# The order of the attention blocks in a two-layer decoder trunk: from 1, 2, 3 to 3, 2, 1

## The chip, the cores and the metric

One core of a Trainium2 chip runs the whole kernel in one launch. The metric is the device time of one execution in microseconds; the kernel before is given by the median of three runs. The engines are TensorE (PE in the profile, PEld for its weight loads), VectorE (DVE), ScalarE (ACT), GpSimd (POOL) and SyncE (SP, which issues the DMAs). Each engine works through its own instructions in a fixed order and waits at an instruction until what it needs is there.

## What is computed

The reference is a decoder trunk of two layers on 512 tokens of width 1024, in float32. Each layer normalises x, projects it once (W_in), gives the columns to three mixers, projects their joined outputs back (W_out), adds them to x, and then adds a squared-ReLU MLP. The mixers are a sparse attention of 8 heads of 64 with 2 key heads, an S5 recurrence and a Mamba-2 recurrence (SSD). The attention works by blocks of 128 queries; block b sees (b+1) x 128 keys:

```python
def attend(args):
    q_b, qi_b, wi_b, start = args
    idx_logits = jnp.einsum('bqhd,bsd->bqhs', qi_b, ki).astype(jnp.float32)
    score = jnp.einsum('bqh,bqhs->bqs', wi_b, jax.nn.relu(idx_logits))
    score = jnp.where(admissible[None], score, -jnp.inf)
    _, sel = lax.top_k(score, topk)      # topk = 128
...
    logits = jnp.where(valid[:, :, None, None, :], logits, -jnp.inf)
    p = jax.nn.softmax(logits, axis=-1).astype(v_sel.dtype)
    o = jnp.einsum('bqgrk,bqkgd->bqgrd', p, v_sel)
```

Blocks don't depend on each other. The 128 best of a block's keys are all of them in block 0, which needs no score.

## The kernel before, in words

Each layer has a stage of mixers and a stage of MLP. In layer 0 the mixers take about the first 330 us and the MLP the time to about 700; layer 1's mixers follow to about 955, then its MLP.

In the mixers' stage `mixers` starts nine or ten generators, each of which emits instructions and yields a cost: `trunk_in` (W_in, in parts kv, xa, qi, q, xb, u5, z; each weight slab is split into a high and a low half, L191 on ACT and L192 on DVE, and each product is three matmuls, L458 to L460), `keys`, `select`, `attention`, two of `recurrent` (S5 and SSD) and three of `out_proj`. `merge` (L1136) runs the generator whose virtual clock is least and adds the yielded cost, scaled by `PLAN`'s `pace`, with offsets from `start` and priorities from `prio`; a scheduler then orders each engine's instructions by priority. So the order in which generators emit blocks, and the places where they must wait for each other, set the order on every engine. PLAN has an entry for each layer.

`keys` (L1284) prepares the keys and then calls `index_scores` (L1058) for the blocks 1, 2, 3: ropes on the block's qi (L1002 to L1005, DVE), a split (L1042 ACT, L1043 DVE), transposes (L1046, PE), and for each of 8 heads two matmuls into `ix` (L1055), a ReLU `irl` (L1071, ACT) and a weighted sum into `isc` (L1073, L1074, L1076, DVE). `select` (L1296) takes the groups of blocks in PLAN's `top`; `topk_masks` (L1081) does 16 rounds for each group, in a round for each of its blocks one MAX8 (L1086) and one MATCH_REPLACE8 (L1087), and turns the scores into a mask (L1090). Layer 0 takes blocks 2 and 1 together and then 3; layer 1 takes 1, 2, 3 one by one.

`attention` (L1305) waits for q and the keys, takes the sums of squares of q (L983 ACT, L984 DVE) and their reciprocal roots, and then for each block ropes and transposes q, waits for the block's mask and calls `attend` (L1092): for each head two matmuls into `lg` (L1055), logits, mask and row maximum in one DVE instruction (L1107, into `pe` and `nmax`), exp (L1108, ACT), normalisation (L1111, L1115 on ACT, L1117 on DVE), then transposes `pTp` (L1123, PE), a copy `pT` (L1125, ACT), the product with v into `po` (L1128, PE), and its high and low half `mh` (L1132, ACT) and `ml` (L1133, DVE). The output projection of the attention part needs the `mh` and `ml` of all four blocks; its sums into x are L1373.

SSD's convolution (L844 to L858, DVE with ACT's tanh) makes `cv` and `CT` from the parts xa and xb; its transposes are L880 (`ssdT`), its scores L893 (`ssds`), both on PE. S5 ends in a gate: L762 and L777 on ACT, L763 and L779 on DVE.

Of the kernel before, what the change touches and what calls it, by code (L numbers as in the profile page):

```python
# [22 lines left out]
NB = S // P  # L23
# [35 lines left out]
PLAN = (  # L59
    {  # L60
        "w_order": ("kv", "xa", "qi", "q", "xb", "u5", "z"),
        "top": ((2, 1), (3,)),
        "out": (("s5",), ("att",), ("ssd",)),
        "serial": "no",
        "norm_act": (0,),
# [5 lines left out]
    },  # L71
    {
        "w_order": ("kv", "xa", "qi", "z", "u5", "q", "xb"),
        "top": ((1,), (2,), (3,)),
        "out": (("s5",), ("att",), ("ssd",)),
        "serial": "no",
        "norm_act": (0,),
# [143 lines left out]
class Net:  # L221
# [1064 lines left out]
    def keys(self, l, r):  # L1286
        while "ksb" not in r:
            yield None
        yield self.start["key"]
        r["K"] = yield from self.attn_keys(l, r["ksb"], self.rt)  # L1290
        for b in (1, 2, 3):
            while b not in r["qi"]:
                yield None
            yield from self.index_scores(b, r["qi"][b], r["K"], r["wi"][:, b], r["acc"])
# [10 lines left out]
    def attention(self, l, r):  # L1305
        nc = self.nc
        while len(r.get("q", ())) < NB or "K" not in r:
            yield None
        yield self.start["att"]
        q, rt = r["q"], self.rt  # L1310
        qms = self.s([P, NB, NH], tag="qms", bufs=1)
        qrs = self.s([P, NB, NH], tag="qrs", bufs=1)
        for b in range(NB):
            self.head_ms(qms[:, b], q[b], NH)
            yield self.pace["q"] * 0.7
        self.rsqrt(qrs.rearrange("p b h -> p (b h)"), qms.rearrange("p b h -> p (b h)"), NB * NH)
        nc.vector.tensor_scalar(qrs, qrs, -ATT_SCALE, None, ALU.mult)
        ah = [self.g(dt=F32R, name="mh") for _ in range(4)]
        al = [self.g(dt=F32R, name="ml") for _ in range(4)]
        for b in range(NB):  # L1320
            self.rope_q(q[b], *rt[2][b])
            qT = self.transpose_heads(q[b])
            yield self.pace["q"] * 2.5
            while b not in r["mask"]:
                yield None
            yield from self.attend(b, qT, r["K"], r["mask"][b], qrs[:, b], ah, al)
        for i in range(4):
            self.tap(f"at_{l}_{i}", ah[i].bitcast(F32)); self.tap(f"atl_{l}_{i}", al[i].bitcast(F32))
        r["mix"]["att"] = list(zip(ah, al))
# [252 lines left out]
```

## Time and profile before

| | us |
|---|---|
| median of 3 runs (lowest, highest) | 1332.07 (1332.04, 1332.51) |
| profiled execution | 1328.87 |
| its span | 1327.1 |
| PE busy in the span | 1218.0 (92%) |
| DVE busy | 885.2 (67%) |
| ACT busy | 549.2 (41%) |
| POOL busy | 169.7 (13%) |
| PE's share of the chain that ended last | 62% |
| DVE's share of it | 19% |

The busy shares are means over unlike stages: in the MLP stages PE has hardly a gap, and nothing else matters there. The chain of work that ended last is followed back from the last instruction, at each step to what released it. DVE's share of it lies in the mixers' stages. The profiled execution was 3.2 us shorter than the median of the runs; durations and places come from it.

### The profile page before, as it was taken

What the parts mean: (1) busy time and instruction counts of PE and PEld (TensorE: products, weight loads), DVE (VectorE), ACT (ScalarE), POOL (GpSimd) and SP (SyncE); (2) the same over time, 40 slices, a digit from 0 to 9 for tenths busy, and PEclk for the clock granted to TensorE, in tenths of its full rate; (3) what the DMA queues carried; (4) which work ended last, traced back from release to release, by engine and by line L of the source; (5) the groups of instructions that cost most, each with busy time, mean ns of one, the idle gap of its engine ahead of it and who ended that gap; (6) DMA issues with size and microseconds to landing.
All of it is one profiled execution on the core that took longest, in us unless ns stands there. A gap on an engine that the chain in (4) does not pass through costs nothing.

```text
span 1327.1 us, 17056 instructions
## 1 busy us (share of the span) xinstructions
PE 1218.0 (92%) x5708; PEld 977.1 (74%) x5708; DVE 885.2 (67%) x2024; ACT 549.2 (41%) x1128; POOL 169.7 (13%) x302
## 2 busy tenths in 40 slices
PE   5678957889999989999999989968999999999998
PEld 5566745458888868888888767754788888888887
DVE  5998999857886545665564699975475445444443
ACT  4245444664543533534443234455254233242331
POOL 2385100000796040000000000000000000000000
PEclk9889988899999999999999989978999999999999
DMA  5132220002567647677644634300323333333332
GB/s 189 40 88 70 74 74 24 9 1 72 148 213 257 214 146 252 224 262 230 227 149 137 219 120 124 120 17 1 111 88 97 101 97 96 96 96 99 100 110 81
DMA packets 139688, 161.64 MB, mean 122 GB/s; under 512 B 18768, under 2 KB 107600, under 8 KB 139600
## 3 DMA queue, kind: packets, MB, share of 16 engines
q1 hardware_dynamic: 139600, 160.55, 38.5%
q8 instruction: 45, 0.74, 0.2%
q14 instruction: 43, 0.35, 0.1%
HBM read 128.29 MB, written 31.03 MB: 120 GB/s over the span
## 4 chain that ended last, share of the span: by engine, by line
PE 62%; DVE 19%; issue 7%; POOL 6%; ACT 4%; DMA 1%; SPq 0%; ACTq 0%; DVEq 0%; POOLq 0%
PE pm L458 18%; PE pm L460 18%; PE pm L459 18%; PE po L1128 3%; DVE isc L1087 2%; DVE mx L1086 2%; DVE isc L1076 2%; PE pTp L1123 1%; DVE pe L1107 1%; DVE wlo L192 1%; DMA wraw<-in_w_in_dram 1%; POOL pt L660 1%; DVE cv L847 1%; ACT pe L1108 1%; POOL pt L661 1%
## 5 line engine op out<-in xcount | busy, mean ns | idle before, releaser
L192 DVE TENSOR_TENSOR wlo<-wraw,whi 128x512 fp32r<-128x512 f32 (+1 forms) x312 | 223.2, 718 | 243.0 <-ACT whi L191 241.4
L191 ACT ACTIVATE whi<-wraw 128x512 fp32r<-128x512 f32 (+1 forms) x312 | 194.1, 625 | 374.5 <-PE pm L459 236.9
L458 PE MATMUL pm<-xh,whi 128*128 128x512 f32 x640 | 252.4, 395 | 3.8 <-ACT q L1224 3.2
L460 PE MATMUL pm<-xh,wlo 128*128 128x512 f32 x640 | 250.1, 392 | 1.2 <-DVE wlo L192 1.2
L459 PE MATMUL pm<-xl,whi 128*128 128x512 f32 x640 | 250.9, 392 | 0.0
L460 PE MATMUL pm<-uh,wlo 128*128 128x512 f32 x512 | 199.7, 390 | 0.3 <-DVE wlo L192 0.3
L458 PE MATMUL pm<-uh,whi 128*128 128x512 f32 x512 | 199.6, 390 | 0.0
L459 PE MATMUL pm<-ul,whi 128*128 128x512 f32 x512 | 199.6, 390 | 0.0
L458 PEld LDWEIGHTS pm<-xh,whi 128*128 128x128 f32 x640 | 120.8, 189 | 30.8 <-ACT q L1224 3.9
L460 PEld LDWEIGHTS pm<-xh,wlo 128*128 128x128 f32 x640 | 120.6, 189 | 27.4 <-DVE wlo L192 2.0
L459 PEld LDWEIGHTS pm<-xl,whi 128*128 128x128 f32 x640 | 121.1, 189 | 24.2 <-issue 0.2
L460 PEld LDWEIGHTS pm<-uh,wlo 128*128 128x128 f32 x512 | 96.2, 188 | 20.8 <-DVE wlo L192 0.9
L459 PEld LDWEIGHTS pm<-ul,whi 128*128 128x128 f32 x512 | 96.3, 188 | 20.4 <-issue 0.4
L458 PEld LDWEIGHTS pm<-uh,whi 128*128 128x128 f32 x512 | 96.2, 188 | 20.3 <-issue 0.4
L458 PE MATMUL pm<-whi,xh 128*128 128x512 f32 (+1 forms) x176 | 67.4, 385 | 14.0 <-ACT xh L392 12.8
L460 PE MATMUL pm<-whi,xl 128*128 128x512 f32 (+1 forms) x176 | 66.6, 380 | 1.3 <-DVE xl L394 1.3
L459 PE MATMUL pm<-wlo,xh 128*128 128x512 f32 (+1 forms) x176 | 67.0, 381 | 0.5 <-DVE wlo L192 0.3
L1408 DVE TENSOR_TENSOR ul<-ur,uh 128x512 fp32r<-128x512 f32 x64 | 48.5, 758 | 21.0 <-ACT uh L1407 21.0
L1406 DVE SCALAR_TENSOR_TENSOR ur<-pm,ur 128x512 f32<-128x512 f32 x64 | 43.9, 686 | 23.0 <-ACT ur L1403 22.7
L1414 DVE TENSOR_TENSOR sq<-pm,r2b 128x512 f32<-128x512 f32 x64 | 44.1, 689 | 17.5 <-PE pm L460 17.5
L1407 ACT ACTIVATE uh<-ur 128x512 fp32r<-128x512 f32 x64 | 39.9, 624 | 30.7 <-DVE ur L1406 30.7
L1087 DVE MATCH_REPLACE8 isc<-mx,isc 128x256 f32<-128x256 f32 (+2 forms) x96 | 51.6, 541 | 0.0
(345 smaller groups left out, 1931.4 us busy)
## 6 DMA issues: line engine op xcount, KB each, us to landing
wraw<-in_w_up_dram SPq DMA_DIRECT2D x128, 256.0 KB, 2.8
wraw<-in_w_down_dram SPq DMA_DIRECT2D x128, 256.0 KB, 2.8
st<-shi SPq DMA_DIRECT2D x48, 256.0 KB, 2.9
st<-slo SPq DMA_DIRECT2D x48, 256.0 KB, 3.5
wlo<-st SPq DMA_DIRECT2D x48, 256.0 KB, 3.0
whi<-st SPq DMA_DIRECT2D x48, 256.0 KB, 2.8
wraw<-in_w_in_dram SPq DMA_DIRECT2D x32, 256.0 KB, 2.8
sraw<-in_w_in_dram SPq DMA_DIRECT2D x32, 256.0 KB, 3.9
```

The source lines that it names most:

```text
L191: nc.scalar.activation(hi, raw, AF.Copy)
L192: nc.vector.tensor_tensor(lo, raw, hi.bitcast(F32), ALU.subtract)
L458: nc.tensor.matmul(p, lh, rh, start=first, stop=False)
L459: nc.tensor.matmul(p, lh, rl, start=False, stop=False)
L460: nc.tensor.matmul(p, ll, rh, start=False, stop=last)
L1076: v.scalar_tensor_tensor(acc, r, wi[:, h:h + 1], acc, ALU.mult, ALU.add)
L1087: v.match_replace(acc, m8, acc, SENT)
L1128: nc.tensor.matmul(po[g_ * 64:g_ * 64 + 64], self.vt[:, kb, g_], pts[g_], start=kb == 0, stop=kb == b)
L1406: v.scalar_tensor_tensor(r, p, 0.0, r, ALU.max, ALU.mult)
L1407: nc.scalar.activation(h, r, AF.Copy)
L1408: v.tensor_tensor(lo, r, h.bitcast(F32), ALU.subtract)
L1414: v.tensor_tensor(t, d[1], rb, ALU.mult)
```

## The change

Three tables or loops get another order. Layer 0's `top` takes block 3 first and then 2 and 1 together; layer 1's takes 3, 2, 1; `keys` scores 3, 2, 1; `attention` takes 0, 3, 2, 1. Paces, starts, priorities and all shapes stay.

```diff
--- before.py
+++ after.py
@@ -59,7 +59,7 @@
 PLAN = (
     {
         "w_order": ("kv", "xa", "qi", "q", "xb", "u5", "z"),
-        "top": ((2, 1), (3,)),
+        "top": ((3,), (2, 1)),
         "out": (("s5",), ("att",), ("ssd",)),
         "serial": "no",
         "norm_act": (0,),
@@ -71,7 +71,7 @@
     },
     {
         "w_order": ("kv", "xa", "qi", "z", "u5", "q", "xb"),
-        "top": ((1,), (2,), (3,)),
+        "top": ((3,), (2,), (1,)),
         "out": (("s5",), ("att",), ("ssd",)),
         "serial": "no",
         "norm_act": (0,),
@@ -1288,7 +1288,7 @@
             yield None
         yield self.start["key"]
         r["K"] = yield from self.attn_keys(l, r["ksb"], self.rt)
-        for b in (1, 2, 3):
+        for b in (3, 2, 1):
             while b not in r["qi"]:
                 yield None
             yield from self.index_scores(b, r["qi"][b], r["K"], r["wi"][:, b], r["acc"])
@@ -1317,7 +1317,7 @@
         nc.vector.tensor_scalar(qrs, qrs, -ATT_SCALE, None, ALU.mult)
         ah = [self.g(dt=F32R, name="mh") for _ in range(4)]
         al = [self.g(dt=F32R, name="ml") for _ in range(4)]
-        for b in range(NB):
+        for b in (0, 3, 2, 1):
             self.rope_q(q[b], *rt[2][b])
             qT = self.transpose_heads(q[b])
             yield self.pace["q"] * 2.5
```

What this does to the order on PE, where layer 0's scores begin. `ix` is a head's score, `pm` the projection's sum, `hT` the transposed qi; the row with - is of before, with + of the change, and the others stand in both.

```order
-L1055 MATMUL ix_1189<-kh_766,hT_1176 128x256
-L1055 MATMUL ix_1189<-kl_767,hT_1176 128x256
+L1055 MATMUL ix_1189<-kh_766,hT_1176 128x512
+L1055 MATMUL ix_1189<-kl_767,hT_1176 128x512
 L460 MATMUL pm_1022<-whi_1201,xl_290 128x512
 L458 MATMUL pm_1046<-whi_1201,xh_288 128x512
 L459 MATMUL pm_1046<-wlo_1202,xh_288 128x512
 L460 MATMUL pm_1046<-whi_1201,xl_290 128x512
-L1055 MATMUL ix_1208<-kh_766,hT_1176 128x256
-L1055 MATMUL ix_1208<-kl_767,hT_1176 128x256
 L458 MATMUL pm_1050<-whi_1201,xh_288 128x512
 L459 MATMUL pm_1050<-wlo_1202,xh_288 128x512
```

The first head stays in its place and is 512 wide instead of 256; the second head, which stood four `pm` matmuls behind it, has moved further back.

DVE in layer 0, up to the first L984. Before (`isc_1188` is block 1's score here, `isc_1320` block 2's, `mx` the eight largest of a round):

```order
L1086 MAX mx_573_2414<-isc_1188 128x8
L1004 TENSOR_TENSOR qi_1014<-qi_1014,cols 128x8x16
L1087 MATCH_REPLACE isc_1188<-mx_573_2414,isc_1188 128x256
L1005 TENSOR_TENSOR qi_1014<-qi_1014,rsw_1599 128x8x16
L1086 MAX mx_578_2429<-isc_1188 128x8
L984 TENSOR_REDUCE qms_1448<-hsq_1450 128x8
L984 TENSOR_REDUCE qms_1448<-hsq_1454 128x8
L985 TENSOR_SCALAR qms_1448<-qms_1448 128x8
```

With the change (`isc_1188` is now block 3's score):

```order
L1076 SCALAR_TENSOR_TENSOR isc_1188<-irl_1384,wd_138,isc_1188 128x512
L1005 TENSOR_TENSOR qi_1009<-qi_1009,rsw_1488 128x8x16
L1002 TENSOR_TENSOR rsw_1748<-qi_1004,cols 128x8x8
L1003 TENSOR_TENSOR rsw_1748<-qi_1004,cols 128x8x8
L1004 TENSOR_TENSOR qi_1004<-qi_1004,cols 128x8x16
L1005 TENSOR_TENSOR qi_1004<-qi_1004,rsw_1748 128x8x16
L984 TENSOR_REDUCE qms_1397<-hsq_1399 128x8
```

The pairs of L1086 and L1087 that stood ahead of L984 are gone from there; its last rows of work are a score of block 3 and ropes. Block 3's eighth and last head, and its first round, stand 39 rows further back with the change:

```order
L1076 SCALAR_TENSOR_TENSOR isc_1188<-irl_1478,wd_138,isc_1188 128x512
L1043 TENSOR_TENSOR hhl_1493<-qi_1009,hhl_1493 128x4x64
L192 TENSOR_TENSOR wlo_1833<-wraw_1692,whi_1832 128x512
L1086 MAX mx_562_2381<-isc_1188 128x8
L1087 MATCH_REPLACE isc_1188<-mx_562_2381,isc_1188 128x512
```

The eighth score now stands behind L984 and what follows from it for q.

DVE in layer 1, at the convolution of xb (`cv_8788` and `cv_8864` of before, `cv_8744` and `cv_8820` with the change). Before:

```order
L1117 TENSOR_SCALAR pe_8658<-pe_8658,psum_8640 128x256
L1117 TENSOR_SCALAR pe_8665<-pe_8665,psum_8640 128x256
L1090 TENSOR_SCALAR isc_7853<-isc_7853 128x512
L1210 TENSOR_TENSOR xb_8766<-pm_8694,rb_7490 128x512
L844 TENSOR_SCALAR cv_8788<-xb_8766,hconvw,hconvb 128x512
L847 SCALAR_TENSOR_TENSOR cv_8788<-xb_8766,hconvw,cv_8788 128x511
L1133 TENSOR_TENSOR ml_8457<-po_8605,mh_8453 128x128
L847 SCALAR_TENSOR_TENSOR cv_8788<-xb_8766,hconvw,cv_8788 128x510
L1133 TENSOR_TENSOR ml_8458<-po_8605,mh_8454 128x128
L847 SCALAR_TENSOR_TENSOR cv_8788<-xb_8766,hconvw,cv_8788 128x509
L1133 TENSOR_TENSOR ml_8459<-po_8605,mh_8455 128x128
L1210 TENSOR_TENSOR xb_8862<-pm_8701,rb_7490 128x512
```

With the change:

```order
L1090 TENSOR_SCALAR isc_7909<-isc_7909 128x256
L1210 TENSOR_TENSOR xb_8818<-pm_8666,rb_7490 128x512
L851 SCALAR_TENSOR_TENSOR cv_8744<-cth_8749,cv_8744 128x512
L844 TENSOR_SCALAR cv_8820<-xb_8818,hconvw,hconvb 128x512
L1373 TENSOR_TENSOR x_123<-x_123,pm_8804 128x512
L847 SCALAR_TENSOR_TENSOR cv_8820<-xb_8818,hconvw,cv_8820 128x511
L847 SCALAR_TENSOR_TENSOR cv_8820<-xb_8818,hconvw,cv_8820 128x510
L847 SCALAR_TENSOR_TENSOR cv_8820<-xb_8818,hconvw,cv_8820 128x509
L857 MEMSET CT_8827 64x512
L857 MEMSET CT_8828 64x512
L1107 ISA pe_8836,nmax_8837<-lg_8833,isc_7703,qrs_8422 128x512
L1107 ISA nmax_8837 128x1
```

The convolution stood behind mask 3 (L1090, 512 wide) among the outputs of block 1; with the change it stands behind mask 1 (256 wide), and an L1107 of block 3 comes between its last sums and L858.

## Rows read from the trace of the kernel before

**Rows 1.** Stretches of layer 0: length, busy us (x instructions) of each engine, PEclk, DMA.

```profile
90.00:120.00 30.00, 25.60 (x129) 20.28 (x127) 24.73 (x42) 13.32 (x30) 27.49 (x52) 1.00 0.24 64
120.00:180.00 60.00, 53.07 (x268) 40.48 (x267) 59.95 (x188) 32.51 (x79) 9.76 (x15) 1.00 0.29 76
180.00:240.00 60.00, 41.19 (x201) 30.45 (x202) 54.75 (x140) 26.42 (x66) 0.00 (x0) 0.77 0.12 40
270.00:300.00 30.00, 25.94 (x138) 16.89 (x138) 17.50 (x49) 18.29 (x46) 0.00 (x0) 0.94 0.00 1
```

**Rows 2.** Stretches of layer 1.

```profile
780.00:810.00 30.00, 23.42 (x113) 18.68 (x113) 30.00 (x82) 10.19 (x26) 0.53 (x1) 0.89 0.46 137
870.00:900.00 30.00, 20.73 (x103) 15.06 (x102) 21.52 (x57) 16.86 (x47) 0.00 (x0) 0.77 0.00 1
```

**Rows 3.** Tile hsq, 120 to 135 us: count, min/median/max ns, first and last start.

```profile
L983 ACT ACTIVATE hsq<-q x4: 662/662/663, 123.1 to 124.6; 128x512 f32<-128x512 f32 x4
L984 DVE TENSOR_REDUCE qms<-hsq x4: 672/682/684, 125.7 to 127.6; 128x8 f32<-128x512 f32 x4
```

**Rows 4.** Top-k rounds of block 1, 110 to 126 us.

```profile
L1086 DVE MAX8 mx<-isc x7: 414/425/429, 114.6 to 125.3; 128x8 f32<-128x256 f32 x7
L1087 DVE MATCH_VALUE_LOAD isc<-mx,isc x6: 79/91/93, 115.0 to 124.7; 128x8 f32 x6
L1087 DVE MATCH_REPLACE8 isc<-mx,isc x6: 404/409/417, 115.1 to 124.8; 128x256 f32<-128x256 f32 x6
```

**Rows 5.** Scores on DVE, blocks 1, 2, 3 (256, 384, 512 wide), and the split of qi.

```profile
L1073 DVE TENSOR_SCALAR isc<-irl,wd x1: 353/353/353, 104.6 to 104.6; 128x256 f32<-128x256 f32 x1
L1076 DVE SCALAR_TENSOR_TENSOR isc<-irl,wd,isc x7: 516/711/834, 105.5 to 113.7; 128x256 f32<-128x256 f32 x7
...
L1073 DVE TENSOR_SCALAR isc<-irl,wd x1: 403/403/403, 119.8 to 119.8; 128x384 f32<-128x384 f32 x1
L1076 DVE SCALAR_TENSOR_TENSOR isc<-irl,wd,isc x5: 595/608/615, 122.6 to 136.6; 128x384 f32<-128x384 f32 x5
...
L1073 DVE TENSOR_SCALAR isc<-irl,wd x1: 474/474/474, 142.0 to 142.0; 128x512 f32<-128x512 f32 x1
L1076 DVE SCALAR_TENSOR_TENSOR isc<-irl,wd,isc x6: 735/743/749, 145.0 to 163.8; 128x512 f32<-128x512 f32 x6
...
L1043 DVE TENSOR_TENSOR hhl<-qi,hhl x2: 653/742/831, 113.0 to 115.9; 128x256 fp32r<-128x256 f32 x2
```

**Rows 6.** Waits of DVE, 90 to 230 us: us in total, times, longest.

```profile
DVE ge L763 <- ACT ge L762: 1.6, 1, 1.6
DVE isc L1076 <- ACT irl L1071: 1.5, 3, 0.7
DVE sig L779 <- ACT sig L777: 1.1, 1, 1.1
```

**Rows 7.** Logits and outputs of blocks 1 to 3 in layer 0.

```profile
L1107 DVE CUSTOM_DVE_ANT_0 pe<-lg,isc,qrs x24: 453/612/752, 228.7 to 278.5; 128x256 f32<-128x256 f32 x8, 128x384 f32<-128x384 f32 x8, 128x512 f32<-128x512 f32 x8
...
L1133 DVE TENSOR_TENSOR ml<-po,mh x12: 271/283/292, 243.6 to 297.3; 128x128 fp32r<-128x128 f32 x12
```

**Rows 8.** Waits of PE, 200 to 345 us.

```profile
PE po L1128 <- ACT pT L1125: 9.7, 5, 6.0
PE pTp L1123 <- ACT pe L1115: 3.9, 4, 1.8
```

**Rows 9.** Waits of DVE, 738 to 868 us.

```profile
DVE rsw L1002 <- ACT qi L1224: 4.3, 1, 4.3
```

**Rows 10.** Waits of PE, 860 to 945 us.

```profile
PE ssds L893 <- DVE CT L858: 4.2, 1, 4.2
PE ssdT L880 <- DVE cv L851: 3.5, 1, 3.5
```

**Rows 11.** Two stretches of layer 1, columns as in the first group.

```profile
872.00:880.00 8.00, 0.89 (x4) 0.36 (x4) 7.26 (x15) 2.91 (x9) 0.00 (x0) 0.67 0.00 0
880.00:888.00 8.00, 7.34 (x33) 6.55 (x34) 4.73 (x11) 4.94 (x15) 0.00 (x0) 0.50 0.00 0
```

## The prediction

> **What bounds the kernel now.** I read the stretches of layer 0's mixers first, then those of layer 1, then the waits inside them. In layer 0 the reader is to see VectorE (DVE) take 59.95 of the 60 us from 120 to 180 us and still 54.75 of the next 60, while TensorE (PE) falls from 53.07 busy us to 41.19 [rows 1]. So DVE sets the pace here: scores, top-k rounds, weight splitting (L192) and the S5 work all stand in its one queue. From 270 us on DVE has only 17.50 of 30: what is left there is the chain logits, softmax, transposes, output, with PE at 25.94. Layer 1 looks alike on a smaller scale: DVE 30.00 in 780 to 810, then 21.52, with PE at 20.73, in 870 to 900 [rows 2]. So time is lost or won in two places: where DVE is full, and in the chain of the three attentions behind it, whose last result frees the dense output projection.
>
> **The change, part by part.** No work is added or taken away: every engine issues the same operations on the same shapes, in another order, and the DMA queue keeps its issues. What can change is only waiting. The sum below goes against the profiled execution, 1328.87 us (span 1327.1 and 1.8 us around it); the median of the runs is 1332.07, 3.2 us above it, and I add those 3.2 at the end.
>
> *Scores of layer 0.* Before, block 1's scores come first. They are narrow, block 1 is ready at once for its top-k rounds, and DVE does such rounds while it waits for the rest. Now block 3 comes first, at double width, its eighth head's score is held back by the plan's pace until after the q projection (the order pieces on DVE in layer 0), and no top-k round can start before it. The next thing on DVE that depends on another engine is L984, the sums of the squares of q. It can't come much earlier than now, as it follows the q projection on PE and two steps on ACT: the first square (L983) starts at 123.1 and takes 0.66, so its result is there at 123.8; L984 now starts at 125.7 [rows 3], 1.9 us later, since DVE was behind.
>
> What DVE had done between the first score and L984 before, and has no longer ahead of L984 now: 7 MAX8 at 0.425 and 6 MATCH_REPLACE8 at 0.409 with their loads at 0.091 make 2.98 + 3.00 = 5.98 us [rows 4]; of block 2, one L1073 at 0.403 and two L1076 at 0.608 make 1.62, and two splits L1043 at 0.742 make 1.48; block 1's L1073 at 0.353 and seven L1076 at 0.711 make 5.33 [rows 5]. That is 14.4 us. In its place stand block 3's L1073 at 0.474 and six L1076 at 0.743: 4.9 [rows 5]. Ropes and weight splits are the same number on both sides. DVE thus comes to L984 with 14.4 - 4.9 = 9.5 us less done. By the least duration in each of the same rows (0.516 for the seven L1076, 0.735 for the six wide ones, and so on) it is 12.7 - 4.9 = 7.8; the medians before 120 us are stretched, as the same L1076 takes from 0.516 to 0.834 while POOL has 27.49 of 30 us [rows 1, 5]. DVE must stand still for it: it waits for the heads of block 3, which leave PE further apart among the projection's matmuls (first order piece), and then for q. What it can win back is the 1.9 us by which it was late. PE worked nearly without a break there, so q comes at most about 1 us earlier. Loss: 7.8 - 1.9 - 1 = 4.9 at the least, 9.5 - 1.9 = 7.6 at the most. I take 6.2, the middle, as the stretched durations hold for a part of that time only.
>
> *Behind it.* The eighth head is scored only after q's split, transposes and copy; DVE waits for it once more. The trace has no such wait; its nearest rows are the waits of L1076 for L1071, 1.5 us in 3, the longest 0.7 [rows 6]. I take 0.7, bounds 0 and 1.5.
>
> *Given back.* S5's steps now stand about 8 us of DVE work further ahead in DVE's order, as the top-k rounds that stood ahead of them have moved behind. Two waits in S5's gate go with that: L763 for ACT 1.6 us, L779 for ACT 1.1 [rows 6]: up to 2.7, at the least 0. I take 2.7, since the DVE work that comes between ACT's step and its reader grows by more than both waits.
>
> *Attention of layer 0.* From the first L1107 of a block to its first L1133 takes 14.9 us for block 1 (228.7 to 243.6), and to the end of the three attentions (the last L1133 starts at 297.3) 68.6 in all [rows 7]. The three pieces follow each other in any order, with the same work in each, so their sum stays. The masks don't gate it: mask 3 stands in DVE's order long before the first L1107 that reads it, and masks 2 and 1 are done just ahead of theirs. What changes is the cover: top-k rounds that ran beside the attention of 1 and 2 now run beside that of 3. I take 0. The bounds are ±4: four waits of PE for the normalised probabilities make 3.9 us [rows 8], and they could all go, or come a second time.
>
> *Layer 1.* The scores of block 3 form one group on PE, and the ropes of the three blocks fill time in which DVE waits anyhow: L1002 waited 4.3 us for ACT's qi copy [rows 9]. What moves is the convolution of xb (the order pieces on DVE in layer 1). Before, it stood behind mask 3, in the tail of block 1's attention, and PE waited 3.5 us for L851 and 4.2 for L858 [rows 10]. Now it stands amid block 3's L1107, with one L1107 and all normalisations behind it. The matmuls that wait for it still come before the second group of block 3's transposes, so I expect the two PE waits to move, not to go. I take 0, bounds ±4 by the longer of them.
>
> *Clock.* PE had 0.89 us of work in the 8 us from 872 to 880, and the granted clock was 0.50, that is 1.2 GHz, in the 8 us behind it, with 7.34 busy us [rows 11], which at 2.4 GHz would be 3.7 less. So a PE wait costs its length and up to half of the work behind it. The Trainium skill ("TensorE: Matmul & The Clock Gate", Part 1) has it as a rule that the throttled clock is the default and activity releases it; by that rule every wait that the new order makes long is paid twice and every long one that it breaks up is won twice, and the stretch agrees with it (0.50 behind 7.1 idle us). It speaks for wider cases on both sides, not for one sign.
>
> *Sum.* 6.2 + 0.7 - 2.7 + 0 + 0 = +4.2: the profiled execution at 1333.1, the median at **1336.3 us**. In the bounds of its first three terms: 4.9 + 0 - 2.7 = +2.2 to 7.6 + 1.5 - 0 = +9.1, before the ±4 of each attention stage.
>
> **Rivals.** *No change* (1332 us, ±2.7, which is the 0.2% that a measurement of this kernel can tell). The 4.2 us that DVE loses by 130 us are taken up later: DVE is idle 12.5 of the 30 us from 270 to 300 [rows 1], and if a chain of PE and ACT alone sets the end of attention, its start need not move. Against it: DVE has 0.05 us idle from 120 to 180, and the S5 output and the first L1107 come out of that queue. 0.20.
>
> *Faster.* In layer 1 the convolution now runs beside block 3's softmax instead of holding PE. If its L858 is done before PE has run out of logits and transposes, both PE waits go, 3.5 + 4.2 = 7.7, and the half clock behind them, 3.7: 11.4 us won in layer 1 against 4.2 lost in layer 0, -7.2 and so 1324.9. It decides at one point: whether the second L858 comes before PE's idle time would begin, 872 us now. For it speaks that the last attention is then block 1's, whose matmuls are fewest; against it that DVE is as far behind there as before. 0.22.
>
> *Much slower.* The attentions of 2 and 1 now follow with less other work on PE between them. One more wait like that of po for pT, the longest 6.0 us [rows 8], and the half clock behind it, 3.7, add 9.7 to the 4.2: 1346. 0.13.
>
> **How the numbers follow.** My forecast, slower by 2.7 to 9.1 us, has 0.45. Slower by over 0.2% is that and the much slower case: 0.58; no change 0.20; faster 0.22. The range reaches down into the faster case, to 1326 (6 us below the median, leaving out some 0.12), and up to 1347, past the much slower case's value (leaving out some 0.06). The forecast's own range is 1334.8 to 1341.2.
>
> **What would show it.** In the new profile L984 of layer 0 should still start at 123 to 126 us, with MAX8 starting only after about 133 instead of 114.6, and waits of DVE on L1071 and L983 of about 8 to 10 us between 104 and 135. The two S5 gate waits should be gone. The last L1133 of layer 0 should start 4 us later, near 301.5, and the interval between the layers' last L1133 should be as before. I am wrong if L984 starts well before 123, if the last L1133 of layer 0 is not later though DVE was, or if the two PE waits for the convolution in layer 1 are gone instead of moved.

## The result

The changed kernel takes 1353.49 us (median of 4 runs, 1352.7 to 1355.82) against 1332.29 us before (4 runs, 1332.04 to 1332.91): ratio 1.0161, 95% interval 1.0146 to 1.0175. It is 21.2 us slower, where +4 us was forecast and the range ended at +15. The sign was right and the size wrong.

The two profiled executions lie further apart than the medians, 1355.82 and 1328.87 us, that is 27 us: the one before was on the short side of its runs, the one after on the long side. Places and waits below come from them, sizes from the medians.

The page of the changed kernel, busy time of PE and DVE with the span:

```profile
span 1354.0 us, 17069 instructions
PE 1232.4 (91%) x5708; PEld 987.4 (73%) x5708; DVE 885.4 (65%) x2024; ACT 548.9 (41%) x1128; POOL 174.3 (13%) x302
```

DVE has the same 885 us as before, ACT and POOL nearly so. PE was busy 1218.0 us in 1327.1 before and 1232.4 in 1354.0 now, with the same 5708 matmuls: 14.4 us more busy, and 121.6 instead of 109.1 us idle. So of the 26.9 us between the spans about half is idle PE and about half is matmuls that took longer. The stretches of layer 0 show the clock at which they ran (columns as in [rows 1]):

```profile
90.00:120.00 30.00, 26.87 (x123) 21.23 (x122) 21.18 (x29) 15.05 (x30) 27.41 (x52) 1.00 0.29 76
120.00:180.00 60.00, 51.12 (x250) 39.89 (x250) 57.21 (x148) 29.33 (x75) 14.79 (x18) 0.92 0.26 71
180.00:240.00 60.00, 41.56 (x210) 31.95 (x208) 56.64 (x156) 23.86 (x54) 0.36 (x1) 0.80 0.09 27
240.00:300.00 60.00, 44.74 (x228) 28.01 (x227) 43.04 (x143) 35.95 (x101) 0.00 (x0) 0.89 0.04 14
```

Against [rows 1] DVE has 21.18 us instead of 24.73 in the stretch of the first scores and 57.21 instead of 59.95 in the next, and the granted clock there is 0.92 instead of 1.00. So DVE is idle 11.6 us from 90 to 180 us, and 5.3 before: 6.3 us more. The first square of q and the first top-k rounds, tiles hsq and mx (mx from 130 to 160 us):

```profile
L983 ACT ACTIVATE hsq<-q x4: 661/662/663, 120.8 to 122.4; 128x512 f32<-128x512 f32 x4
L984 DVE TENSOR_REDUCE qms<-hsq x4: 674/676/677, 125.6 to 127.5; 128x8 f32<-128x512 f32 x4
...
L1086 DVE MAX8 mx<-isc x4: 685/688/695, 138.8 to 147.8; 128x8 f32<-128x512 f32 x4
```

L984 stands at 125.6, where [rows 3] have 125.7, as forecast. But the first square of q started at 120.8 instead of 123.1, so DVE came to L984 about 4.1 us after its input was there, and 1.9 before: it did not wait for q. Ahead of L984 stand block 3's first scores, tile isc from 105 to 126 us:

```profile
L1076 DVE SCALAR_TENSOR_TENSOR isc<-irl,wd,isc x6: 764/1116/1572, 108.5 to 122.9; 128x512 f32<-128x512 f32 x6
```

They took 1.12 us in the median, where the same shape took 0.743 later in the stage before [rows 5], and POOL was busy 27.41 of the 30 us up to 120. What stretched them was not tested. The first round has moved from 114.6 [rows 4] to 138.8; the forecast was after about 133. What DVE waited for from 90 to 230 us (the view of [rows 6]):

```profile
DVE isc L1076 <- ACT irl L1071: 4.3, 3, 2.1
DVE wlo L192 <- ACT whi L191: 3.2, 3, 1.5
DVE sig L779 <- ACT sig L777: 1.8, 1, 1.8
```

The wait for the heads' scores is there, 4.3 us instead of 1.5, and a wait of the weight split behind it. The 8 to 10 us of waits for L1071 and L983 that the forecast had are not: none was for L983. The gate's L763 has gone from the list, as forecast, but L779 waits 1.8 us instead of 1.1.

The attentions: a stretch from the end of block 0's last L1133 to the end of the last block's, first the kernel before, then the changed one, layer 0 and layer 1 of each:

```profile
223.20:297.60 74.40, 62.21 (x327) 39.88 (x325) 54.96 (x161) 47.21 (x128) 0.00 (x0) 0.93 0.05 15
855.10:938.30 83.20, 66.38 (x339) 44.27 (x339) 54.72 (x154) 47.62 (x127) 0.00 (x0) 0.88 0.06 20
```

```profile
232.60:312.70 80.10, 63.32 (x317) 39.63 (x316) 55.29 (x178) 45.26 (x124) 0.00 (x0) 0.87 0.05 14
877.60:965.10 87.50, 69.29 (x352) 46.06 (x351) 55.12 (x158) 47.40 (x127) 0.00 (x0) 0.88 0.08 25
```

Layer 0 comes to its attentions 9.4 us later and then needs 5.7 us more for them; layer 1 needs 4.3 us more. DVE's work in a stretch is the same to 0.4 us. From the end of layer 0's last L1133 to that of layer 1's it is 652.4 us now and 640.7 before, where "as before" was forecast.

### The profile page after: what moved, and what is told of

The parts are those of the page before. It is cut to its first block, busy times and chain, and to the rows that moved or that the text cites. A ratio compares the mean times of both kernels' runs of the same rounds, so it can differ in the third digit from the quotient of the medians.

```text
span 1354.0 us, 17069 instructions
## 1 busy us (share of the span) xinstructions
PE 1232.4 (91%) x5708; PEld 987.4 (73%) x5708; DVE 885.4 (65%) x2024; ACT 548.9 (41%) x1128; POOL 174.3 (13%) x302
## 4 chain that ended last, share of the span: by engine, by line
PE 71%; DVE 18%; ACT 4%; issue 4%; DMA 1%; POOL 1%; SPq 0%; ACTq 0%; DVEq 0%; POOLq 0%
PE pm L458 21%; PE pm L460 21%; PE pm L459 20%; PE po L1128 3%; DVE isc L1087 2%; DVE mx L1086 2%; PE pTp L1123 2%; DVE isc L1076 1%; ACT pe L1108 1%; DVE pe L1107 1%; DVE cv L847 1%; DVE wlo L192 1%; DMA wraw<-in_w_in_dram 1%; PE hTp L1046 1%; PE ssdy L907 1%
## 5 line engine op out<-in xcount | busy, mean ns | idle before, releaser
L1087 DVE MATCH_REPLACE8 isc<-mx,isc 128x384 f32<-128x384 f32 (+2 forms) x96 | 51.6, 541 | 0.0
```

The costliest lines, as they stand in the source:

```text
L1087: v.match_replace(acc, m8, acc, SENT)
```

## The experiments

All times are medians, and each difference is taken to the runs of the kernel before on the same chip (1331.4 to 1332.3 us). The few lines that an edit changes are shown against the kernel before, or against the kernel named; lines left out are marked by three dots.

**Which layer.** `l0_only`: layer 0 as changed, layer 1 as before (`l1_only` is the other way round, with layer 1's `top` as changed):

```diff
-        "top": ((2, 1), (3,)),
+        "top": ((3,), (2, 1)),
...
-        for b in (1, 2, 3):
+        for b in ((3, 2, 1), (1, 2, 3))[l]:
...
-        for b in range(NB):
+        for b in ((0, 3, 2, 1), (0, 1, 2, 3))[l]:
```

> Layer 0 has the new order (scores 3, 2, 1; top-k 3, then 2 and 1; attention 0, 3, 2, 1), layer 1 the old one. Theory (both layers pay, each in its own waits): the last L1133 of layer 0 comes 13 to 16 us later than before, the kernel is 12 to 16 us slower (1344 to 1348). Rival (all of the loss arises in layer 0, layer 1 only carries it): 20 to 22 us slower, 1352 to 1354.

> Layer 1 has the new order, layer 0 the old one. Theory: 5 to 9 us slower (1337 to 1341), with S5's wait of PE for X in layer 1 (7.4 us in the changed kernel) there as well. Rival (layer 1 only carries a delay): no change, within 2 us of 1332.

Measured: 1345.34 us, +13.7 (ratio 1.0097, 1.008 to 1.0114), and 1338.43, +6.8 (1.0048, 1.0033 to 1.0063). Together +20.5, nearly the whole 21.2: the layers pay separately, and the rival falls.

**Layer 0, the spacing of the heads.** A head's cost grows with its block's number, so the merge sets block 3's heads further apart than block 1's. `l0_dense_heads` gives every head of layer 0 the cost of a head of block 1 ("dense heads"), against `l0_only`:

```diff
-            yield self.pace["idx"] * (0.25 + 0.2 * b)
+            yield self.pace["idx"] * (0.25 + 0.2 * (1 if self.plan is PLAN[0] else b))
```

> As l0_only, but in layer 0 every head's score yields the cost of a block-1 head (0.45 instead of 0.25 + 0.2 b), so that block 3's eight heads come as close on PE as block 1's do before. Theory (DVE stands still in the scores because the heads come late and no top-k round is ready): first MAX8 at 114 to 118 us instead of 138.8, the last L1133 of layer 0 7 to 9 us earlier than in l0_only, the kernel 6 to 9 us faster than l0_only. Rival (the order of the attentions costs it): within 2 us of l0_only.

Measured: 1338.03 us, +6.4 to before and 7.3 less than `l0_only`. Rounds and outputs in its trace, tiles mx (110 to 126 us) and ml (226 to 320), and then the ml row of `l0_only` (232 to 320):

```profile
L1086 DVE MAX8 mx<-isc x3: 683/687/695, 118.1 to 123.6; 128x8 f32<-128x512 f32 x3
...
L1133 DVE TENSOR_TENSOR ml<-po,mh x12: 280/284/292, 253.5 to 305.0; 128x128 fp32r<-128x128 f32 x12
```

```profile
L1133 DVE TENSOR_TENSOR ml<-po,mh x12: 274/283/292, 260.6 to 311.8; 128x128 fp32r<-128x128 f32 x12
```

The first round starts at 118.1, where it is 138.8 in the changed kernel, and the last output 6.8 us earlier than in `l0_only`. The control, `old_order_dense`, makes the same edit alone in the kernel before:

> The kernel before with dense heads in layer 0 (0.45 for every head) alone. Theory (dense heads help only where DVE has no top-k round to do between the heads): within 2 us of before. Rival (dense heads are better in any order): 4 us faster or more.

Measured: 1331.3 us, -0.3 (0.9988 to 1.0006). Dense heads help only in the new order, so the 7.3 us are what the spread heads cost there. The edit closes up block 2's heads too; block 3's share alone was not run.

**Layer 0, the attentions.** Seven runs looked for the other 6 us. `l0_attention_swap` changes the order of the small blocks alone; the second edit is `l0_dense_0312`, against `l0_dense_heads`:

```diff
-        for b in range(NB):
+        for b in ((0, 2, 1, 3), (0, 1, 2, 3))[l]:
...
-        for b in ((0, 3, 2, 1), (0, 1, 2, 3))[l]:
+        for b in ((0, 3, 1, 2), (0, 1, 2, 3))[l]:
```

> Only the attention of layer 0 has another order, 0, 2, 1, 3; scores and top-k stay as before, so that the masks of 2 and 1 are both ready before either is used. Theory (the order of attentions costs little by itself, some 3 us by a wait between two blocks): 0 to 4 us slower. Rival (the order of the attentions is the main cost): 6 us slower or more.

Measured: 1333.29 us, +1.6 (0.9998 to 1.0017), not told from no change.

> l0_dense_heads with the last two attentions of layer 0 exchanged: 0, 3, 1, 2; scores and top-k stay (3, then 2 and 1). From the end of block 0's last L1133 to the end of the last one takes 74.4 us before and 79.6 in l0_dense_heads. Theory (the smaller the last block, the longer the stage, as nothing else is left to run beside its waits): about 77, the kernel 2 to 3 us faster than l0_dense_heads. Rival (block 3's place at the front costs, whatever comes last): 79 to 80, the kernel within 1 us of l0_dense_heads.

Measured: 1339.33 us, 7.4 over before and not faster than `l0_dense_heads`; the stretch is 80.0 us:

```profile
227.40:307.40 80.00, 62.74 (x317) 39.36 (x315) 53.69 (x172) 45.83 (x124) 0.00 (x0) 0.87 0.05 14
```

My theory of the small last block falls: with block 3 in front the stretch is as long with block 2 last as with block 1 last. `l0_0231` was to show the same from the other side (top-k `((2,), (3,), (1,))`, attention 0, 2, 3, 1):

> The kernel before with layer 0's top-k in the order 2, 3, 1 one by one and attention 0, 2, 3, 1; scores stay 1, 2, 3. Theory (the last block's size decides): the stretch between the ends of block 0's and of the last attention 79 to 80 us. Rival (block 3 at the front decides): 75 to 77 us, as with 0, 2, 1, 3 (75.6). The kernel's time takes in what the top-k rounds lose ahead of that, and tells less.

Measured: 1342.16 us, +10.2, stretch 84.9. It settles nothing: L1090, which makes mask 3, started at 260.7 only, and block 3's logits began at 261.3, 10.9 us after block 2's last output had ended, so the stretch holds a wait for top-k that I hadn't foreseen.

These runs have one wait of PE in the stretch in common, that of L1123 for the normalised probabilities of L1115: 3.9 us before, 3.6 in `l0_attention_swap` and 3.9 in `old_order_dense`, where block 3 is last; 6.9 in the changed kernel, 7.3 in `l0_only`, 7.2 in `l0_dense_heads` and 6.3 in `l0_dense_0312`, where it is in front. `l0_0231`, with block 3 in the middle, has 4.7.

Four runs moved other work. `l0_dense_ssd0` and `old_order_ssd0` set SSD's start in layer 0 from -7 to 0, `l0_dense_out8` and `old_order_out8` the output projection's pace from 1.504 to 8; SSD's edit:

```diff
-        "start": {"tab": 0.5, "key": 5.0, "top": 41.0, "att": 0.0, "s5": 12.0, "ssd": -7.0, "out": 20.0},
+        "start": {"tab": 0.5, "key": 5.0, "top": 41.0, "att": 0.0, "s5": 12.0, "ssd": 0.0, "out": 20.0},
```

> l0_dense_heads with SSD's start in layer 0 moved from -7 to 0, so that PE's order has between a block's last transposed q and its first logits only three transposes and two scores of SSD, and no longer a whole chunk (scores, eight ssdy and the state) that waits for DVE. Theory (what is left of layer 0's loss, some 6 us, is these hand-overs between attentions): the last L1133 of layer 0 4 to 6 us earlier than in l0_dense_heads, the kernel 1332 to 1335. Rival (the attention of 3, 2, 1 is longer by itself, for lack of cover): within 2 us of l0_dense_heads.

> The kernel before with SSD's start in layer 0 at 0 alone: now block 3's hand-over has the eight ssdy and the state in front of its logits, which the second hand-over of the changed kernel has too. Theory (such a hand-over costs 1 to 2 us where DVE has its inputs ready): 1 to 3 us slower than before. Rival (SSD's start 0 is better in any order, and l0_dense_ssd0 gains by that and not by the hand-over): 2 us faster or more.

Measured: 1342.04 us (+10.7) and 1338.28 (+6.9). Both theories miss: SSD's later start costs about as much as the change's remainder in the old order as well. The two orders differ by 3.8 us then. What the hand-overs (from one block's outputs to the next block's logits) cost by themselves is not shown by these two. The wait of L1123 is 1.8 us in `l0_dense_ssd0` and 3.1 in `old_order_ssd0`, so it hangs on SSD's place too, and its going did not make the stretch shorter.

> The kernel before with the pace of the output projection in layer 0 at 8 instead of 1.5: block 1's logits come 26 rows earlier on PE, and S5's 48 output matmuls stand spread among the attentions, where PE is idle 12 us in the kernel before. Theory (the attentions wait for hand-overs, and PE has time to give there): 3 to 8 us faster than before. Rival (the matmuls push each hand-over back by as much): within 2 us, or slower.

> l0_dense_heads with the pace of the output projection in layer 0 at 8. Theory (the new order lacks other work beside the last, small attentions): 5 to 9 us faster than l0_dense_heads, and no more than 2 us from old_order_out8. Rival (cover is not the point): the distance from old_order_out8 stays at 5 to 7 us.

Measured: 1333.93 us (+2.3) and 1336.67 (+5.1). Filling PE's idle time among the attentions makes the old order slower. The new one is 1.4 us faster than `l0_dense_heads`, which the spread of these runs (1336.06 to 1340.06 against 1334.31 to 1337.48) does not tell from no change. The distance between the orders falls from 6.4 to 2.7 us, mostly because the old one loses. The wait of L1123 stays apart, 7.7 us against 2.7. So it is not shown that the new order suffers for lack of cover, that is of other work for PE beside the attentions' waits.

**Layer 1.** `l1_top_start10` is `l1_only` with top-k's start in layer 1 at 10 instead of 15:

> l1_only with the start of top-k in layer 1 at 10 instead of 15. In DVE's order 12.2 us of top-k rounds then stand between S5's last u5 and its last X, as before the change (l1_only: 21.2 us). Theory (layer 1's loss is that X comes late, behind wide rounds): X within 2 us of before, PE's wait for X below 4 us, the kernel 4 to 6 us faster than l1_only, 1332 to 1335. Rival (the loss lies in the attentions or at the convolution): within 2 us of l1_only.

Measured: 1339.39 us, +8.0. X did come back (PE's wait for it fell from 7.4 to 0.2 us), and nothing was won; PE waited 5.9 us for a transfer of S5's u5 (`U<-u5d`) instead, 1.5 in `l1_only`. Taking the wait for X away by itself is no mending. `l1_order_132` takes layer 1 in the order 1, 3, 2 throughout (scores, `top` and attention, of which the last is shown), `l1_0213` changes its attention alone:

```diff
-        for b in range(NB):
+        for b in ((0, 1, 2, 3), (0, 1, 3, 2))[l]:
...
-        for b in range(NB):
+        for b in ((0, 1, 2, 3), (0, 2, 1, 3))[l]:
```

> Layer 1 in the order 1, 3, 2 (scores, top-k, attention after block 0), layer 0 as before. Block 1's short attention is then done before the convolution of xb, as before the change, and only 3 and 2 change places. Theory (layer 1's loss of 6.8 us in l1_only is that block 3's logits share DVE with the convolution, where the old order has a short attention done ahead of it): at most 2.5 us slower than before. Rival (a small block at the end costs, with no other work beside it, whatever stands at the convolution): 4 us slower or more.

> Only the attention of layer 1 has another order, 0, 2, 1, 3; scores and top-k stay. In layer 0 the same exchange cost 1.6 us. Here the order on DVE puts the convolution of xb ahead of block 2's logits, so that no attention is done before it. Theory (layer 1 pays for what of the attentions is left when the convolution ends: 56.7 us from there to the last L1133 with block 1 done before it, 64 to 68 with block 3 begun): 66 us or more from the convolution's end, the kernel 5 to 12 us slower than before. Rival (the place of the small blocks matters little, as in layer 0): within 2 us of before.

Measured: 1339.04 us (+7.4) and 1343.2 (+11.2; 1.0059 to 1.0093). The first missed in its total, the second came out as the theory had it. Tiles CT (the end of the convolution) and ml show both, in the order before, `l1_only`, `l1_order_132`, `l1_0213`:

```profile
L858 DVE SCALAR_TENSOR_TENSOR CT<-cth,cv x2: 620/654/689, 879.8 to 880.8; 64x512 f32<-64x512 f32 x2
L1133 DVE TENSOR_TENSOR ml<-po,mh x12: 282/290/292, 872.3 to 938.0; 128x128 fp32r<-128x128 f32 x12
```

```profile
L858 DVE SCALAR_TENSOR_TENSOR CT<-cth,cv x2: 678/684/689, 882.2 to 882.9; 64x512 f32<-64x512 f32 x2
L1133 DVE TENSOR_TENSOR ml<-po,mh x12: 281/283/292, 896.7 to 947.7; 128x128 fp32r<-128x128 f32 x12
```

```profile
L858 DVE SCALAR_TENSOR_TENSOR CT<-cth,cv x2: 619/653/687, 887.6 to 888.6; 64x512 f32<-64x512 f32 x2
L1133 DVE TENSOR_TENSOR ml<-po,mh x14: 282/290/292, 862.2 to 948.8; 128x128 fp32r<-128x128 f32 x14
```

```profile
L858 DVE SCALAR_TENSOR_TENSOR CT<-cth,cv x2: 620/656/691, 874.2 to 874.9; 64x512 f32<-64x512 f32 x2
L1133 DVE TENSOR_TENSOR ml<-po,mh x12: 281/292/292, 901.9 to 953.6; 128x128 fp32r<-128x128 f32 x12
```

From the start of the second L858 to that of the last L1133 it is 57.2 us before, 64.8 in `l1_only`, 60.2 and 78.7. Before, block 1's outputs start at 872.3: that block is done when the convolution ends. In `l1_only` the outputs of block 3 start at 896.7, so only its logits are done by then; in `l1_order_132` block 1 is done again (its four L1133 start at 879.5 to 882.2; the row begins with two of block 0), and in `l1_0213` nothing is (block 2's outputs start at 901.9). PE's waits for the convolution are the same there, 3.7 us for L851 and 4.2 for L858 against 3.5 and 4.2 [rows 10], so it isn't a longer wait at the convolution that costs the 11.2 us. From block 0's last L1133 to the last of all `l1_0213` takes 95.0 us instead of 83.2, for 339 matmuls in both: 72.5 busy us at a granted clock of 0.82, where it was 66.4 at 0.88, and the rest is PE idle. In `l1_order_132` the convolution ended 7.7 us later, which took back what it won; why was not traced. `l1_0312` (against `l1_only`, attention 0, 3, 1, 2) leaves the state at the convolution as it is there:

> l1_only with the attentions of layer 1 in the order 0, 3, 1, 2; scores and top-k stay 3, 2, 1. The same stretch takes 83.2 us before, 88.1 in l1_only. Theory: 85 to 86, 2 to 3 us faster than l1_only. Rival: 88, within 1 us of l1_only.

Measured: 1341.63 us, +9.7 and not faster than `l1_only`; its stretch is 91.3 us. So the theory of what is done ahead of the convolution rests on `l1_0213` and on the rest in `l1_order_132` (60.2 us); no run mends layer 1 by it.

**The three numbers together.** `all_three_mended` is the whole change with dense heads, SSD's start 0 and top-k's start 10:

> The whole change with the three numbers: dense heads and SSD's start 0 in layer 0, top-k's start 10 in layer 1. Theory (three separate waits, whose costs add): within 4 us of before, 1330 to 1336. Rival (the order itself costs): more than 8 us slower than before.

Measured: 1347.98 us, +16.6. Two of the three numbers were no mending.

**Without most of top-k.** `old_one_round` and `new_one_round` (the new order in both layers, dense heads in layer 0) leave out 15 of the 16 rounds:

```diff
-        for it in range(16):
+        for it in range(1):
```

> The kernel before with one top-k round instead of 16 for each block in both layers (left out: the other 15, so the masks keep 8 keys instead of 128). It is the base for new_one_round: both theories expect it 40 to 90 us faster, since DVE loses about 100 us of rounds, and the stretch from block 0's last L1133 to the last one shorter than before in both layers, 60 to 74 us in layer 0 and 65 to 83 in layer 1.

> Scores, top-k and attention in the order 3, 2, 1 in both layers, dense heads in layer 0, and one top-k round instead of 16 for each block (15 left out). Theory (the 5 us that the attentions lose in each layer come from top-k rounds that stand in DVE's queue among them): the stretch of attentions within 2 us of old_one_round's in each layer. Rival (attention and SSD by themselves are slower with block 3 in front): 4 to 6 us longer than old_one_round's in each layer.

Measured: 1316.61 us (15.0 less than before) and 1330.73, 14.1 us apart. With all rounds the sum of `l0_dense_heads` and `l1_only` is 6.4 + 6.8 = 13.2. Page of the old order, then its stretches in layers 0 and 1; then those of the new order:

```profile
span 1314.0 us, 16793 instructions
PE 1214.0 (92%) x5708; PEld 974.5 (74%) x5708; DVE 802.5 (61%) x1754; ACT 549.6 (42%) x1128; POOL 168.5 (13%) x302
...
221.10:294.80 73.70, 59.40 (x317) 37.35 (x316) 43.45 (x133) 46.36 (x126) 0.00 (x0) 0.95 0.05 15
845.00:925.10 80.10, 67.83 (x360) 45.01 (x359) 53.74 (x149) 48.09 (x127) 0.00 (x0) 0.94 0.10 33
```

```profile
223.60:302.00 78.40, 61.27 (x310) 38.17 (x309) 42.78 (x129) 45.31 (x124) 0.00 (x0) 0.89 0.05 14
850.00:940.10 90.10, 73.37 (x360) 48.79 (x359) 53.53 (x149) 47.59 (x127) 0.00 (x0) 0.87 0.09 30
```

DVE has 82.7 us less work, and the kernel gains 15 where I expected 40 to 90. And with one round for each block the new order still costs 4.7 us in layer 0's stretch and 10.0 in layer 1's, there more than the rival's 4 to 6. The theory of the rounds falls: attention and SSD by themselves are slower so. In layer 0 PE's wait of L1123 for L1115 is 6.4 us again, against 4.3. In layer 1, 5.5 of the 10.0 us are PE busy longer on the same 360 matmuls at a granted clock of 0.87 instead of 0.94, the rest is PE idle.

## Why the prediction was right or wrong

The sum's terms that failed are these: of the 21.2 us, the two attention stages, taken at 0 each, made about 6.0 and 6.8, and the start of layer 0's attentions 8.5, where 4.2 was forecast.

*What bounds the kernel.* The step "So DVE sets the pace here" failed. DVE was full, but much of it was rounds that fill its time: taking 82.7 us of them out gave 15. In layer 0 DVE was then busy 95.9 of the 131.1 us from 90 us to the end of block 0's last L1133, where it had been 124.6 of 133.2, and that end came only 2.1 us earlier. With DVE and PE both idle in part, a chain of waits between the engines sets this stage, and I had PE's idle time only as a consequence. The Trainium skill ("Perfetto Trace Analysis", Identifying the Most-Contended Engine) has it that the engine of the highest occupancy is the most contended and is to be optimized first; in the stretch from 120 to 180 us that would be DVE by this rule, and here the measurement decides against it: an engine can be full of work that has time.

*Scores of layer 0.* The place was right: DVE stood still where the scores came far apart, and closing the heads up gave 7.3 us back. Forecast: 6.2 + 0.7 - 2.7 = +4.2 at the start of the attentions. In `l0_only`, which has layer 1 as before, block 0's last L1133 ends 8.5 us later (231.7 against 223.2), with dense heads 2.5 later (225.7). The loss was sized about right: DVE's idle time from 90 to 180 us grew by 6.3 us, where 6.2 + 0.7 was forecast. The term that failed is the 2.7 us given back: one gate wait went, 1.6 us, the other grew by 0.7, and what makes up the distance to 8.5 stays open. That L984 kept its place was luck in part. The prediction had DVE waiting there for q, but q came 2.3 us earlier, not at most 1, and DVE came later than q, after waits and after wide scores that took 1.12 us where the prediction had 0.743 from later rows. Of the 6.3 us about half were waits for the heads (4.3 + 0.8 us for L1071, before 1.5 + 0.5).

*Attention of layer 0.* "I take 0", since the sum of the pieces stays, failed: +6.0 in `l0_only` (80.4 us, 231.7 to 312.1), 4.7 with one top-k round. The sum depends on the order: with block 3 in front the stretch is 78.4 us (one round) to 80.4, without it 73.7 to 75.6 as long as SSD and the output projection keep their places, and neither which block is last nor the rounds make it by themselves. In the changed kernel PE is idle 16.8 us of the stretch instead of 12.2, and 3.0 of these 4.6 us are the waits for the normalised probabilities, 6.9 instead of 3.9. The prediction had named just these as its bound ("or come a second time") and left them out of the sum. Why they grow with block 3 in front stays open.

*Layer 1.* "I expect the two PE waits to move, not to go. I take 0" failed as well, with +6.8; in `l1_only` 4.9 of it lie in the stretch of attentions (88.1 us against 83.2). The order piece on DVE showed what I now think mattered, the convolution among block 3's logits; I read it as a wait that moves and didn't ask what of the attentions is done ahead of it. Before, that is a whole block, with the change only block 3's logits. `l1_0213` is the clearest sign: with block 3 still last and scores and top-k untouched, it is 11.2 us slower when nothing is done before the convolution. It is the likeliest cause and not a shown one, since bringing block 1 back ahead of the convolution (`l1_order_132`) did not win the time back.

*Clock.* I left it out of the sum, as it spoke for both signs. It is half of the difference of the profiles: 14.4 us of busy PE on the same matmuls. The two profiles agree with the Trainium skill ("TensorE: Matmul & The Clock Gate", Part 1), by which activity releases the clock: more idle PE went with a lower granted clock, 0.953 over the whole span against 0.967. Idle time in sum does not settle it: `l1_only` has PE idle 115.5 us, 6.4 more than before, at 0.967 as well.

*The rivals.* No change and faster are out; the two PE waits at the convolution became 0.7 and 5.4 us in layer 1 (the second grew), but nothing was won by it. The much slower case, 1346 us, came nearest, with waits between the attentions and a lower clock behind them; it had 0.13. Its place was right and its wait was not: from 200 us on in layer 0 the wait of `po` for `pT` stayed about as in [rows 8], and that for the normalised probabilities rose from 3.9 to 6.9 us:

```profile
PE po L1128 <- ACT pT L1125: 10.3, 4, 5.7
PE pTp L1123 <- ACT pe L1115: 6.9, 4, 2.5
```

Its cause, missing cover, was not borne out: `l0_dense_out8`, which gave cover, is not told from `l0_dense_heads`.

## What to carry to other kernels

An engine that is full isn't the bound if part of its work is filler: ask which of its instructions somebody waits for, and try a run without the rest before pricing them. When equal pieces change places beside a second chain on the same engine, the sum of the pieces need not stay; look at each fixed event (here a convolution) for what is done ahead of it and what is left behind it. A virtual cost that sets spacing by block size, as the heads' cost here, can be harmless in one order (-0.3 us without it) and cost 7.3 us in another; look at both together. A place that comes out as forecast can do so for another reason, as L984's did: compare when its input was there.

## What the runs showed of the hardware

Longer waits of PE went with slower matmuls: between `old_one_round` and `new_one_round` the same 360 matmuls of layer 1's stretch, equal in number for each line and shape, took 67.83 and 73.37 us, at a granted clock of 0.94 and 0.87, with 12.3 and 16.7 us of idle PE. Moving a wait without shortening the stage can go with a lower clock too: `l1_top_start10` has PE busy 1225.6 us at 0.958 over the span, against 1221.4 at 0.967 in `l1_only`. The same wide score instruction (L1076, 512 wide) took 1.12 us in the median up to 123 us of the changed kernel, beside a busy POOL, and 0.743 after 145 us of the kernel before [rows 5].
